# The second half of an output projection, computed one token tile at a time ahead of an expert gather

## The chip, the cores and the metric

One core of a Trainium2 chip runs the whole kernel. Its engines are TensorE (PE: matmuls and, as PEld, weight loads), VectorE (DVE), ScalarE (ACT), GpSimd (POOL) and SyncE (SP, which here only issues transfers). Each engine works through its own queue strictly in order, and semaphores tie the queues together. The metric is device time in microseconds (us). Times in the rows are counted from the start of the profiled span.

## The reference

Two transformer-like blocks follow each other on 256 tokens of 1024 features. The end of the first block is what matters here:

```python
x = x + mixed @ w_out[l]                                  # output projection, 1024 x 1024
x = x + peer_ffn(rmsnorm(x, norm2_gain[l]), peer_w_query[l], ...)
# peer_ffn, for blocks of 128 tokens:
q = (xb @ w_query).reshape(t, 8, 2, 64)                   # 8 heads, two half queries each
s = einsum('thpd,hpkd->thpk', q, sub_keys)                # scores against 128 keys per half
top_s, top_i = top_k(s, 16)                               # 16 best of each half,
best_s, best_pos = top_k(sums of all pairs, 16)           # then the 16 best pairs
u, vv = expert_down[idx], expert_up[idx]                  # 16 rows of 1024 each, per token and head
out = (softmax(best_s) * gelu(xb . u)) @ vv
```

For every token and head, 16 rows of `expert_down` and `expert_up` are fetched from memory, at places known only once the token's scores are sorted. So the fetch of the first head's experts needs the whole row of x for its 128 tokens: the output projection, the norm, the first queries, the scores and the sort.

## The kernel before, in words

The 256 tokens are two tiles of 128 tokens (tile 0 and tile 1 below). Activations are kept transposed (features on partitions) as pairs of rounded halves, `hi` and `lo`. A float32 product is three matmuls (`mm3`, L122: `lh x rl`, `ll x rh`, `lh x rh`). Weights come from memory in chunks of 512 KB, two slices of 128 features by 512 columns. A chunk lands in a buffer `raw` (pool `st`, three buffers), ACT rounds it into `hi` (L106) and DVE writes the difference into `lo` (L110). When DVE has done so, the `raw` buffer is free for SP's next transfer. `stream` (L112) puts `hi` and `lo` into small rings (four and three buffers), which matmuls have to release. These transfers and splits carry a high priority in the scheduler that orders each engine's queue at compile time; equal priorities keep the order of the program.

The stretch around the change runs in this order. `mix_b` ends the first stage (context c1) and writes `mTh`, `mTl`, the input of the output projection. Context c2 then opens its pools `gp`, `wp` and `rt` in the memory that c1's pool gives back. In `gp` lies a ring of ten buffers of 8 KB a partition (`ring`, L697, tag "ga"). Two of them hold the transposed x (`rTh`, `rTl`), four hold the split first half of the query weights (`wh`, `wl`), and the expert rows are gathered into the same ten buffers as they come free.

The output projection (L703 to L707) goes by halves of 512 columns, n = 0 and n = 1. For each half, four chunks of `w_out` are streamed, each used for both token tiles: 48 matmuls of 128x512 a half. VectorE adds the sums to x, and `n2.half(n)` (L224) transposes the four new feature slices of both tiles (L215), writes `rTh` on ACT (L220) and `rTl` on DVE (L221), and has ACT square x for the norm (L247). After n = 1, `n2.factor` (L250) makes the norm factor of both tiles, a chain of small DVE instructions. The split of the query weights' first half (L711 to L717, four chunks of `peer_wq`) keeps its parts in the ring.

Then `lower(0)` (L849) computes tile 0's first queries with 24 matmuls, and `queries` copies them (L732), transposes them (L735) and copies them again (L736). `scores(0, 0)` (L745, L747) and `route(0, 0)` (L752 to L789, on DVE) follow, up to the first list of indices, `idx`. From then on POOL issues indirect gathers of 1 MB (L824), 256 in all, sixteen for each of eight heads and two tiles. `lower(1)`, the second half of the query weights (L866 to L877) and the other scores run beside the first gathers. Each gathered row block is used by a dot product on DVE (L831) and by two matmuls (L840), and then its buffer is free. `after(a, b)` is an edge for the scheduler alone: `a` is queued behind `b` on the same engine.

`tile_part` (L230), which the kernel uses later for the second block's norm, does the transposing and splitting for one token tile and four feature slices, through one PSUM bank.

Of the kernel before, what the change touches and what calls it, by code (L numbers as in the profile page):

```python
# [10 lines left out]
F32 = mybir.dt.float32  # L11
# [6 lines left out]
ALU = mybir.AluOpType  # L18
# [3 lines left out]
P = 128  # L22
D = 1024
KD = D // P
EPS = 1e-6
NEG = -1.0e30
PRIO = 100000
# [4 lines left out]
RAWB, HIB, LOB = 3, 4, 3  # L32
# [15 lines left out]
def peer_hybrid_kernel(ctx: ExitStack, tc: tile.TileContext, A: dict, out: bass.AP, dbg=None, stop=None):  # L48
    nc = tc.nc
    V, S, G, T = nc.vector, nc.scalar, nc.gpsimd, nc.tensor  # L50
    dbg = dbg or {}

    def dump(name, ap):
        if name in dbg:
            nc.gpsimd.dma_start(dbg[name], ap)

    kp = ctx.enter_context(tc.tile_pool(name="kp", bufs=1))
    st = ctx.enter_context(tc.tile_pool(name="st", bufs=1))
    ps = ctx.enter_context(tc.tile_pool(name="ps", bufs=4, space=PSUM))

    def bank(tag="sm"):
        return ps.tile([P, 512], F32, tag=tag, name=tag, bufs=4 if tag == "acc" else 2)
# [8 lines left out]
    x = kp.tile([P, 2, D], F32, name="x", tag="xs")  # L71
# [7 lines left out]
    ident, iota = cst[:, 0], cst[:, 1]  # L79
# [16 lines left out]
    def after(later, earlier):  # L96

        tc.add_manual_dep(later.ins, earlier.ins.name, mybir.DependencyInfo(
            mybir.DependencyClass.NoSync, mybir.DependencyReason.DATA))
# [5 lines left out]
    def split(dst_h, dst_l, src, eng=None):  # L105
        S.activation(dst_h, src, AF.Copy)  # L106
        if eng is None:
            eng = lo_pat[0][cnt[0] % len(lo_pat[0])]
            cnt[0] += 1
        return (V if eng == "v" else G).tensor_tensor(dst_l, src, dst_h.bitcast(F32), op=ALU.subtract)  # L110
# [11 lines left out]
    def mm3(o, lh, ll, rh, rl, start, stop, behind=None):  # L122
        m = T.matmul(o, lh, rl, start=start, stop=False)  # L123
        if behind is not None:
            after(m, behind)
        T.matmul(o, ll, rh, start=False, stop=False)  # L126
        return T.matmul(o, lh, rh, start=False, stop=stop)  # L127
# [38 lines left out]
    def proj_tok(*a, **kw):  # L166
        for _ in proj_tok_steps(*a, **kw):
            pass
# [17 lines left out]
    def rsqrt(dst, ss, inv_n, pool, tag):  # L186
        n = ss.shape[-1]
        shp = list(ss.shape)
        v = pool.tile(shp, F32, tag=tag + "v", name="rsv", bufs=2)
        a = pool.tile(shp, F32, tag=tag + "a", name="rsa", bufs=2)  # L190
        V.tensor_scalar(v, ss, inv_n, EPS, op0=ALU.mult, op1=ALU.add)
        V.tensor_scalar(dst.bitcast(I32), v.bitcast(I32), 1, None, op0=ALU.logical_shift_right)
        V.tensor_scalar(dst.bitcast(I32), dst.bitcast(I32), -1.0, float(0x5F3759DF), op0=ALU.mult, op1=ALU.add)
        for _ in range(3):
            V.tensor_tensor(a, v, dst, op=ALU.mult)
            V.scalar_tensor_tensor(a, a, -0.5, dst, op0=ALU.mult, op1=ALU.mult)
            V.scalar_tensor_tensor(dst, a, 1.5, dst, op0=ALU.add, op1=ALU.mult)

    class Norm:
# [44 lines left out]
        def square(self, tt, halves=(0, 1)):  # L244
            for hf in halves:
                junk = self.pool.tile([P, 512], BF, tag=self.jt[0], name="junk", bufs=self.jt[1])
                after(S.activation(junk, self.x[:, tt, hf * 512:hf * 512 + 512], AF.Square,  # L247
                                   accum_out=self.ss[:, tt, hf:hf + 1]), self.h)

        def factor(self, squares=(), row=True):  # L250

# [76 lines left out]
    with ExitStack() as c1:  # L328
# [22 lines left out]
        acc = [bank("acc") for _ in range(2)]  # L351
        for kc in range(4):
# [4 lines left out]
            for tt in range(2):  # L357
                s = slice(tt * P, tt * P + P)
                for k2 in range(2):
                    k = kc * 2 + k2  # L360
# [96 lines left out]
        b = bank()  # L457
# [5 lines left out]
        for tt in range(2):  # L463
            head_norm(q[:, tt], 16, 64, qg8, b1, "hq")
            rope(q[:, tt], 16, tt, "q")
            for k4 in range(2):
                b = bank()
# [217 lines left out]
    with ExitStack() as c2:  # L685
# [11 lines left out]
        def ring(name, dt=F32R):  # L697
            return gp.tile([P, 2048], dt, tag="ga", name=name, bufs=GB)


        rTh, rTl = (ring(nm).rearrange("p (k t) -> p k t", k=KD) for nm in ("rTh", "rTl"))
        n2 = Norm(x, par("g2"), rt, rTh, rTl)
        for n in range(2):  # L703
            cs_ = slice(n * 512, (n + 1) * 512)
            proj_tok(A["w_out"], n, mTh, mTl, KD,
                     lambda tt, a: V.tensor_tensor(x[:, tt, cs_], x[:, tt, cs_], a, op=ALU.add))
            n2.half(n)  # L707
        n2.factor(row=False)
        dump("x2", x)

        wh, wl = ([ring(f"{nm}{i}") for i in range(2)] for nm in ("wh", "wl"))  # L711
        for kc in range(4):
            raw = st.tile([P, 1024], F32, tag="raw", name="raw", bufs=RAWB)
            o = slice(kc % 2 * 1024, kc % 2 * 1024 + 1024)
            with tc.high_priority(offset=PRIO):
                nc.sync.dma_start(raw, A["peer_wq"][0, kc])
                split(wh[kc // 2][:, o], wl[kc // 2][:, o], raw, "v")  # L717


        idx = [[wp.tile([P, 16], I32, name=f"idx{tt}{h}") for h in range(8)] for tt in range(2)]  # L720
        gate = [[wp.tile([P, 16], F32, name=f"gate{tt}{h}") for h in range(8)] for tt in range(2)]
# [7 lines left out]
        def queries(tt, n, acc):  # L729

            q_ = rt.tile([P, 512], F32, name="q_", bufs=1)
            S.activation(q_, acc, AF.Copy)  # L732
            b = bank()
            for u in range(4):
                T.transpose(b[:, u * P:(u + 1) * P], q_[:, u * P:(u + 1) * P], ident)  # L735
            S.activation(qqT[:, n * 4:n * 4 + 4, tt * P:(tt + 1) * P], b.rearrange("p (h t) -> p h t", h=4), AF.Copy)  # L736

        def scores(tt, n):

            for p_ in range(2):  # L740
                b = bank()
                pr = slice(p_ * 64, p_ * 64 + 64)
                for u in range(4):
                    h = n * 4 + u
                    m = T.matmul(b[:, u * P:(u + 1) * P], qqT[pr, h, tt * P:(tt + 1) * P], keys[pr, h], start=u == 0,  # L745
                                 stop=u == 3)
                c = S.activation(sc[tt][:, n * 4:n * 4 + 4, p_], b.rearrange("p (h k) -> p h k", h=4), AF.Copy,  # L747
                                 scale=n2.r[:, tt:tt + 1])
            return m, c
# [94 lines left out]
        def normalised(tt):  # L844
            xa = S.activation(xn[:, tt], x[:, tt], AF.Copy, scale=n2.r[:, tt:tt + 1])
            after(V.tensor_tensor(xn[:, tt], xn[:, tt], g2r, op=ALU.mult), first)
            return xa

        def lower(tt, behind=None):  # L849
            a = bank("acc")  # L850
            s_ = slice(tt * P, tt * P + P)
            for k in range(KD):
                o = slice(k % 4 * 512, k % 4 * 512 + 512)
                mm3(a, rTh[:, k, s_], rTl[:, k, s_], wh[k // 4][:, o], wl[k // 4][:, o], k == 0, k == KD - 1, behind)
            queries(tt, 0, a)


        lower(0)
        with tc.high_priority(offset=PRIO):
            s0, known = scores(0, 0)  # L860
        with tc.high_priority(offset=PRIO):
            first = route(0, 0, sc[0])
        after(normalised(0), known)
        lower(1, s0)
        acc = [bank("acc") for _ in range(2)]
        for kc in range(4):  # L866
# [449 lines left out]
```

## Time and profile before

| what | value |
|---|---|
| time before, median of 3 runs | 1348.73 us (1348.51 to 1352.42) |
| the profiled execution | 1345.1 us, with a span of 1343.3 us |
| PE, DVE busy over the span | 88%, 67% |
| ACT, POOL busy over the span | 38%, 38% |
| HBM traffic | 285 GB/s over the span |
| expert gathers (queue q0) | 268.45 MB of 383.56 MB moved |

The profiled execution is one run of the program on the chip. In a timeline row the columns are the start, the duration, the engine, the line of the kernel, the operation, its output and inputs by the program's names, and in brackets how long the engine sat idle before it and what ended that wait. In a row of a stretch the columns are the stretch and its length, each engine's busy time with the count of its instructions, the granted clock of TensorE as a share of full speed, the busy share of the transfer engines, and GB/s. SPq and ACTq are the transfers that SP and ACT issue.

### The profile page before, as it was taken

To read this page: it belongs to the slowest core of one execution; us is meant where nothing else is said; L and a number is where in the kernel's file an instruction comes from. 1 tells how busy PE (TensorE), PEld (TensorE's weight loads), DVE (VectorE), ACT (ScalarE), POOL (GpSimd) and SP (SyncE) were. 2 spreads that over 40 slices of the span, in tenths; PEclk is the share of its full clock that TensorE was granted. 3 is DMA by queue.
4 is the path that set the end of the run, shared out by engine and by line. 5 is a ranking of instruction groups with operands and counts; after the bars stand their busy time and mean duration, and the time that the engine had idled before them with its cause. 6 is when DMAs were issued, how large, how long until landed. Compare 5 with 4: busy or idle time off the path is not lost.

```text
span 1343.3 us, 16519 instructions
## 1 busy us (share of the span) xinstructions
PE 1180.3 (88%) x5707; PEld 816.2 (61%) x5707; DVE 894.0 (67%) x1980; ACT 515.4 (38%) x933; POOL 516.8 (38%) x374
## 2 busy tenths in 40 slices
PE   8999999988787778678778777887999999899998
PEld 6977789965333333233333333333888999899987
DVE  6955848677766677776767776665799786635431
ACT  6565535453222122222222222211674564544442
POOL 3322313014454444444445445452100012287964
PEclk9999999989899999999898889889999999999999
DMA  6544425639999999999999999999645346465664
GB/s 217 179 160 128 137 83 163 226 128 427 427 426 427 427 427 427 427 425 427 394 426 427 418 416 426 421 422 385 193 155 172 110 125 192 139 188 179 200 207 136
DMA packets 69779, 383.56 MB, mean 286 GB/s; under 512 B 8000, under 2 KB 8512, under 8 KB 36928
## 3 DMA queue, kind: packets, MB, share of 16 engines
q0 software_dynamic: 36864, 268.45, 47.7%
q1 hardware_dynamic: 31968, 112.15, 27.0%
q10 hardware_dynamic: 864, 1.90, 0.4%
q8 instruction: 46, 0.75, 0.2%
q14 instruction: 37, 0.30, 0.1%
HBM read 381.42 MB, written 1.05 MB: 285 GB/s over the span
## 4 chain that ended last, share of the span: by engine, by line
PE 44%; DMA 26%; DVE 16%; POOL 6%; issue 6%; ACT 2%; POOLq 0%; SPq 0%; DVEq 0%; ACTq 0%
DMA ga<-in_peer_du_dram,idx 23%; PE acc L123 11%; PE acc L126 11%; PE acc L127 11%; DVE jk L831 6%; POOL ga L824 4%; PE acc L840 2%; POOL lo L110 2%; PE sm L1133 1%; PE sm L126 1%; DMA raw<-in_w_fu_dram 1%; PE sm L123 1%; PE sm L127 1%; ACT hi L106 1%; DVE lo L110 1%
## 5 line engine op out<-in xcount | busy, mean ns | idle before, releaser
L840 PE MATMUL acc<-ga,dg 128*128 128x512 f32 x1024 | 489.8, 636 | 132.5 <-ACT dg L837 132.4
L840 PEld LDWEIGHTS acc<-ga,dg 128*128 128x128 f32 x1024 | 203.6, 203 | 416.8 <-issue 236.8
L824 POOL DMA_INDIRECT ga<-in_peer_du_dram,idx x256 | 297.3, 1161 | 386.9 <-PE acc L840 213.9
L831 DVE SCALAR_TENSOR_TENSOR jk<-ga,xn 128x1024 bf16<-128x1024 f32 x253 | 309.4, 1223 | 179.0 <-DMA ga<-in_peer_du_dram,idx 178.6
L106 ACT ACTIVATE hi<-raw 128x1024 fp32r<-128x1024 f32 (+1 forms) x202 | 212.2, 1053 | 235.3 <-PE acc L127 62.7
L110 POOL TENSOR_TENSOR lo<-raw,hi 128x1024 fp32r<-128x1024 f32 (+1 forms) x68 | 166.2, 2449 | 353.3 <-PE acc L127 208.8
L110 DVE TENSOR_TENSOR lo<-raw,hi 128x1024 fp32r<-128x1024 f32 (+1 forms) x134 | 176.7, 1320 | 122.1 <-ACT hi L106 44.0
L123 PE MATMUL acc<-T1l,hi 128*128 128x256 f32 x384 | 107.6, 281 | 2.1 <-DVE T1l L241 2.1
L126 PE MATMUL acc<-T1h,lo 128*128 128x256 f32 x384 | 107.8, 281 | 0.0
L127 PE MATMUL acc<-T1h,hi 128*128 128x256 f32 x384 | 106.9, 279 | 0.0
L123 PE MATMUL acc<-lo,T1h 128*128 128x512 f32 (+1 forms) x256 | 99.2, 395 | 3.1 <-DVE lo L110 1.7
L126 PE MATMUL acc<-hi,T1l 128*128 128x512 f32 (+1 forms) x256 | 99.8, 390 | 0.8 <-DVE T1l L221 0.8
L127 PE MATMUL acc<-hi,T1h 128*128 128x512 f32 (+1 forms) x256 | 99.2, 388 | 0.0
L123 PEld LDWEIGHTS acc<-T1l,hi 128*128 128x128 f32 x384 | 72.2, 188 | 3.0 <-DVE T1l L241 2.4
L126 PEld LDWEIGHTS acc<-T1h,lo 128*128 128x128 f32 x384 | 72.3, 188 | 1.1 <-issue 1.0
L127 PEld LDWEIGHTS acc<-T1h,hi 128*128 128x128 f32 x384 | 72.1, 188 | 0.4 <-issue 0.2
L123 PEld LDWEIGHTS acc<-lo,T1h 128*128 128x128 f32 x256 | 48.1, 189 | 14.0 <-DVE lo L110 2.4
L126 PEld LDWEIGHTS acc<-hi,T1l 128*128 128x128 f32 x256 | 48.5, 190 | 11.0 <-issue 1.1
L127 PEld LDWEIGHTS acc<-hi,T1h 128*128 128x128 f32 x256 | 48.5, 190 | 9.9 <-issue 0.3
L126 PE MATMUL sm<-fhTh,lo 128*128 128x256 f32 x176 | 49.3, 281 | 0.1
L123 PE MATMUL acc<-fhTl,hi 128*128 128x256 f32 x176 | 48.4, 279 | 1.0 <-DVE fhTl L221 1.0
L127 PE MATMUL sm<-fhTh,hi 128*128 128x256 f32 x176 | 49.2, 280 | 0.0
(870 smaller groups left out, 1935.1 us busy)
## 6 DMA issues: line engine op xcount, KB each, us to landing
raw<-in_w_in_dram SPq DMA_DIRECT2D x92, 512.0 KB, 3.6
raw<-in_w_fg_dram SPq DMA_DIRECT2D x22, 512.0 KB, 3.7
raw<-in_w_fu_dram SPq DMA_DIRECT2D x22, 512.0 KB, 3.6
raw<-in_w_fd_dram SPq DMA_DIRECT2D x22, 512.0 KB, 3.7
raw<-in_w_out_dram SPq DMA_DIRECT2D x16, 512.0 KB, 4.4
raw<-in_w_ba_dram SPq DMA_DIRECT2D x8, 512.0 KB, 3.5
raw<-in_w_bm_dram SPq DMA_DIRECT2D x8, 512.0 KB, 3.7
raw<-in_peer_wq_dram SPq DMA_DIRECT2D x8, 512.0 KB, 4.4
```

The source lines that it names most:

```text
L106: S.activation(dst_h, src, AF.Copy)
L110: return (V if eng == "v" else G).tensor_tensor(dst_l, src, dst_h.bitcast(F32), op=ALU.subtract)
L123: m = T.matmul(o, lh, rl, start=start, stop=False)
L126: T.matmul(o, ll, rh, start=False, stop=False)
L127: return T.matmul(o, lh, rh, start=False, stop=stop)
L824: G.indirect_dma_start(ga, None, A["peer_du"], bass.IndirectOffsetOnAxis(idx[tt][h][:, r0 + j:r0 + j + 1], 0))
L831: dot = V.scalar_tensor_tensor(jk, ga[:, 0:D], 1.0, xn[:, tt], op0=ALU.mult, op1=ALU.mult, accum_out=s_[:, j:j + 1])
L840: T.matmul(uacc[tt][dh], dg[:, j], rows[j][:, D + dh * 512:D + dh * 512 + 512], start=h + r0 + j == 0, stop=h == 7 and r0 + j == 15)
L1133: T.matmul(b[:, tt * 4 + m], xl_[:, m, tt], xr_[:, m, tt, :, 1], start=tt + m == 0, stop=tt + m == 4)
```

## The change

The first half of the output projection, n = 0, stays as it is. After it:

- the four chunks of the query weights come first on SP's queue, and `n2.half(0)` stands behind them;
- the second half of `w_out` is no longer streamed through the small rings. Its four chunks are split into four more buffers of the ring of ten (`oh`, `ol`) and stay there;
- `outs(0)` multiplies tile 0 alone (24 matmuls), and `summed(0)` adds it to x, transposes and splits tile 0's four slices by `tile_part`, and squares them. `factor_of(0)` makes tile 0's norm factor;
- `lower(0)`, now at high priority, gives tile 0's first queries. Tile 1's 24 matmuls (`outs(1)`) are queued in three parts: slice 0 behind the last matmul of `lower(0)`, slice 1 behind the transposes of the queries, slices 2 to 7 behind the last matmul of the scores;
- `summed(1)` follows, without an edge (its argument `behind` is not used in it); `factor_of(1)` is queued behind `first`, the cast that writes the first index list; then `lower(1)` as before.

```diff
+        def factor_of(self, tt, behind=None):
+            s = self.pool.tile([P, 2], F32, tag="nst", name="nst", bufs=1)[:, 0:1]
+            a = V.tensor_tensor(s, self.ss[:, tt, 0:1], self.ss[:, tt, 1:2], op=ALU.add)
+            if behind is not None:
+                after(a, behind)
+            rsqrt(self.r[:, tt:tt + 1], s, 1.0 / D, self.pool, "n")
...
+        oh, ol = ([ring(f"{nm}{i}") for i in range(2)] for nm in ("oh", "ol"))
         rTh, rTl = (ring(nm).rearrange("p (k t) -> p k t", k=KD) for nm in ("rTh", "rTl"))
         n2 = Norm(x, par("g2"), rt, rTh, rTl)
-        for n in range(2):
-            cs_ = slice(n * 512, (n + 1) * 512)
-            proj_tok(A["w_out"], n, mTh, mTl, KD,
-                     lambda tt, a: V.tensor_tensor(x[:, tt, cs_], x[:, tt, cs_], a, op=ALU.add))
-            n2.half(n)
-        n2.factor(row=False)
+        proj_tok(A["w_out"], 0, mTh, mTl, KD,
+                 lambda tt, a: V.tensor_tensor(x[:, tt, 0:512], x[:, tt, 0:512], a, op=ALU.add))
...
+        n2.half(0)
+        for kc in range(4):
+            raw = st.tile([P, 1024], F32, tag="raw", name="raw", bufs=RAWB)
+            o = slice(kc % 2 * 1024, kc % 2 * 1024 + 1024)
+            with tc.high_priority(offset=PRIO):
+                nc.sync.dma_start(raw, A["w_out"][1, kc])
+                split(oh[kc // 2][:, o], ol[kc // 2][:, o], raw, "v")
+        oacc = [bank("acc") for _ in range(2)]
+        def outs(tt, ks, behind=None):
+            s_ = slice(tt * P, tt * P + P)
+            for k in ks:
+                o = slice(k % 4 * 512, k % 4 * 512 + 512)
+                m = mm3(oacc[tt], mTh[:, k, s_], mTl[:, k, s_], oh[k // 4][:, o], ol[k // 4][:, o], k == 0, k == KD - 1,
+                        behind)
+            return m
+        def summed(tt, behind=None):
+            V.tensor_tensor(x[:, tt, 512:1024], x[:, tt, 512:1024], oacc[tt], op=ALU.add)
+            n2.tile_part(tt, 1)
+            n2.square(tt, (1,))
+        outs(0, range(KD))
+        with tc.high_priority(offset=PRIO):
+            summed(0)
+            n2.factor_of(0)
...
-        lower(0)
+        with tc.high_priority(offset=PRIO):
+            low, low_t = lower(0)
+        outs(1, (0,), low)
+        outs(1, (1,), low_t)
         with tc.high_priority(offset=PRIO):
             s0, known = scores(0, 0)
+        outs(1, range(2, KD), s0)
+        summed(1, known)
         with tc.high_priority(offset=PRIO):
             first = route(0, 0, sc[0])
         after(normalised(0), known)
+        n2.factor_of(1, first)
         lower(1, s0)
```

`queries` now returns its last transpose and `lower` the last matmul with it, for these edges.

## Rows read from the trace of the kernel before

**Rows 1.** The page: the span, and the transfer engines' busy tenths in 40 slices.
```profile
span 1343.3 us, 16519 instructions
DMA  6544425639999999999999999999645346465664
```
**Rows 2.** Five stretches, all engines.
```profile
251.70:262.70 11.00, 11.00 (x51) 9.10 (x51) 8.28 (x12) 5.35 (x6) 0.00 (x0) 1.00 0.73 240
262.70:274.50 11.80, 11.80 (x58) 9.78 (x57) 7.73 (x11) 6.69 (x12) 0.00 (x0) 1.00 0.61 213
282.20:294.90 12.70, 8.71 (x48) 6.78 (x48) 9.76 (x47) 8.72 (x13) 0.00 (x0) 0.96 0.00 0
297.20:300.70 3.50, 3.50 (x8) 2.81 (x9) 3.50 (x5) 0.00 (x0) 2.75 (x3) 0.50 0.86 290
306.00:936.00 630.00, 494.09 (x1088) 210.01 (x1088) 432.26 (x1142) 146.94 (x399) 288.96 (x250) 0.93 1.01 423
```
**Rows 3.** Timeline of POOL, first and ninth gather.
```profile
295.82 1.21 POOL L824 DMA_INDIRECT ga<-in_peer_du_dram,idx  x1 [55.00 <-DVE idx L789]
...
312.02 0.93 POOL L824 DMA_INDIRECT ga<-in_peer_du_dram,idx  x1 [4.70 <-PE acc L127]
```
**Rows 4.** Timeline of PE: projection, tile 0's queries, transposes, second half of the queries.
```profile
251.74 0.40 PE L123 MATMUL acc<-lo,T1h 128*128 128x512 f32 x1
...
274.46 0.39 PE L123 MATMUL acc<-wl,rTh 128*128 128x512 f32 x1
...
277.19 1.03 PE L215 MATMUL sm<-cst,x 128*128 128x128 f32 x8
...
297.19 0.80 PE L123 MATMUL acc<-lo,rTh 128*128 128x512 f32 x1 [4.16 <-DVE lo L872]
```
**Rows 5.** Timeline of ACT, PE and DVE, from tile 0's queries to the first index list.
```profile
282.18 0.60 ACT L732 ACTIVATE q__3102<-acc 128x512 f32<-128x512 f32 x1 [0.99 <-PE acc L127]
...
282.83 0.66 PE L735 MATMUL sm<-cst,q__3102 128*128 128x128 f32 x4 [0.69 <-ACT q__3102 L732]
...
284.18 1.71 PE L745 MATMUL sm<-keys,qqT 64*128 64x128 f32 x16 [0.69 <-ACT qqT L736]
...
294.70 0.17 DVE L789 CAST idx<-cd__3155 128x16 int32<-128x16 f32 x1
```
**Rows 6.** Timeline of ACT and DVE: weight splits, and where one stage gives way to the next.
```profile
254.93 1.06 ACT L106 ACTIVATE hi<-raw 128x1024 fp32r<-128x1024 f32 x1 [0.35 <-DMA raw<-in_w_out_dram]
...
257.68 0.33 ACTq L690 DMA_DIRECT2D keys<-in_peer_keys_dram  x1
258.12 1.06 ACT L106 ACTIVATE hi<-raw 128x1024 fp32r<-128x1024 f32 x1 [1.54 <-DVE T1l L310]
...
256.96 0.69 DVE L310 SCALAR_TENSOR_TENSOR T1l<-gt,T1h 128x512 fp32r<-128x512 f32 x1
257.56 1.22 DVE L110 TENSOR_TENSOR lo<-raw,hi 128x1024 fp32r<-128x1024 f32 x1
...
276.43 1.22 DVE L110 TENSOR_TENSOR wl<-raw,wh 128x1024 fp32r<-128x1024 f32 x1 [0.27 <-ACT wh L106]
```
**Rows 7.** The buffers `raw` from 235 to 300 us: transfer times.
```profile
DMA to landing us min/median/max: 3.4/4.4/6.8
```
**Rows 8.** Timeline of PE, ACT and DVE: `tile_part` where the kernel uses it later.
```profile
629.26 0.66 PE L235 MATMUL sm<-cst,x 128*128 128x128 f32 x4
...
948.33 0.62 ACT L240 ACTIVATE T1h<-sm 128x128 fp32r<-128x128 f32 x2 [0.17 <-DVE T1l L241]
949.12 0.63 ACT L240 ACTIVATE T1h<-sm 128x128 fp32r<-128x128 f32 x2 [0.16 <-DVE T1l L241]
...
948.73 0.61 DVE L241 SCALAR_TENSOR_TENSOR T1l<-sm,T1h 128x128 fp32r<-128x128 f32 x2 [0.18 <-ACT T1h L240]
```
**Rows 9.** Timeline of DVE: adding the projection, first and last instruction of the norm factor.
```profile
275.48 0.68 DVE L706 TENSOR_TENSOR x<-x,acc 128x512 f32<-128x512 f32 x1
...
281.22 0.16 DVE L255 TENSOR_TENSOR nst<-nss 128x2 f32<-128x2 f32 x1 [0.87 <-ACT junk L247]
...
283.60 0.16 DVE L197 SCALAR_TENSOR_TENSOR nr<-rsa,nr 128x2 f32<-128x2 f32 x1
```

More of the change, by code (lines that the diff above doesn't have):

```diff
@@ L698, in ring @@
             return gp.tile([P, 2048], dt, tag="ga", name=name, bufs=GB)
+        oh, ol = ([ring(f"{nm}{i}") for i in range(2)] for nm in ("oh", "ol"))
         rTh, rTl = (ring(nm).rearrange("p (k t) -> p k t", k=KD) for nm in ("rTh", "rTl"))
         n2 = Norm(x, par("g2"), rt, rTh, rTl)
-        for n in range(2):
-            cs_ = slice(n * 512, (n + 1) * 512)
-            proj_tok(A["w_out"], n, mTh, mTl, KD,
-                     lambda tt, a: V.tensor_tensor(x[:, tt, cs_], x[:, tt, cs_], a, op=ALU.add))
-            n2.half(n)
-        n2.factor(row=False)
-        dump("x2", x)
+        proj_tok(A["w_out"], 0, mTh, mTl, KD,
+                 lambda tt, a: V.tensor_tensor(x[:, tt, 0:512], x[:, tt, 0:512], a, op=ALU.add))
         wh, wl = ([ring(f"{nm}{i}") for i in range(2)] for nm in ("wh", "wl"))
@@ L734, in queries @@
             for u in range(4):
-                T.transpose(b[:, u * P:(u + 1) * P], q_[:, u * P:(u + 1) * P], ident)
+                t = T.transpose(b[:, u * P:(u + 1) * P], q_[:, u * P:(u + 1) * P], ident)
             S.activation(qqT[:, n * 4:n * 4 + 4, tt * P:(tt + 1) * P], b.rearrange("p (h t) -> p h t", h=4), AF.Copy)
+            return t
         def scores(tt, n):
@@ L853, in lower @@
                 o = slice(k % 4 * 512, k % 4 * 512 + 512)
-                mm3(a, rTh[:, k, s_], rTl[:, k, s_], wh[k // 4][:, o], wl[k // 4][:, o], k == 0, k == KD - 1, behind)
-            queries(tt, 0, a)
-        lower(0)
+                m = mm3(a, rTh[:, k, s_], rTl[:, k, s_], wh[k // 4][:, o], wl[k // 4][:, o], k == 0, k == KD - 1, behind)
+            return m, queries(tt, 0, a)
+        with tc.high_priority(offset=PRIO):
+            low, low_t = lower(0)
+        outs(1, (0,), low)
+        outs(1, (1,), low_t)
         with tc.high_priority(offset=PRIO):
             s0, known = scores(0, 0)
+        outs(1, range(2, KD), s0)
+        summed(1, known)
         with tc.high_priority(offset=PRIO):
```

## The prediction

> **What bounds the kernel now.** I read the page first. From about a fifth to seven tenths of the span the transfer engines are full [rows 1]. The stretch table says the same of the expert gathers: from 306 to 936 us the transfer share is 1.01 at 423 GB/s, while TensorE shows a granted clock of 0.93 and idle time [rows 2]. That stage moves a fixed number of bytes at a full rate. So it ends as much earlier or later as it starts, and the question is when it starts. POOL's timeline answers: the first gather is issued at 295.82, after 55 us in which POOL waited for the first index list [rows 3]. The list is written at 294.70 [rows 5]. Everything that the change moves lies on the path to that cast or beside it.
>
> Back from there, tile 0's query copy starts at 282.18, and 12.52 us of copies, transposes, scores and sorting follow [rows 5]. Ahead of it TensorE is the limit: in 251.70 to 274.50 it is busy all the time at a clock of 1.00 [rows 2], with 96 projection matmuls from 251.74 until the query matmuls begin at 274.46 [rows 4]. Weights arrive in time; the transfer share in those two stretches is 0.73 and 0.61 [rows 2].
>
> One matmul of 128x512 costs 0.2275 us in a stream: twelve query matmuls go from 274.46 to the transposes at 277.19 [rows 4]. The 0.39 in their rows is mostly overlap.
>
> **The change, part by part.** Removed from the path are tile 1's 24 matmuls of the second half, 24 x 0.2275 = 5.5 us, tile 1's four slices and its squares. If TensorE stayed the limit, that would be the gain. I think it does not, because the weights become late.
>
> *The weights.* Before the query copy, the path still needs eight chunks after the first half's four: four of the query weights, and now last, four of `w_out`. Their parts no longer wait for matmuls to free a small ring, but they still pass through three `raw` buffers: a transfer, ACT's rounding, DVE's difference, then the next transfer. One such turn is 4.4 us of transfer (median) [rows 7] + 1.06 + 1.22 [rows 6] = 6.7 us for three chunks, 2.2 us a chunk. With the shortest transfer, 3.4 us [rows 7], it is 1.9. What the kernel before achieved for its last eight chunks, with ring waits and queue order in it, is from 257.56 to 276.43 in seven steps [rows 6], 2.7 us a chunk. I take 2.2, and 1.9 and 2.7 as ends.
>
> [...]
>
> *Where the eight begin.* In the kernel before, the first of the eight goes into the small ring and is rounded at 254.93 [rows 6]. Now it goes into a buffer of context c2. The first instruction that touches that context's pools, the transfer of the keys, is issued at 257.68, right after the last instruction of the stage before ends (256.96 + 0.69), and ACT's rounding behind it, at 258.12, is shown waiting for that same instruction [rows 6]. So I let the first rounding start at 258.12: +1.06 + 1.22 = 260.4 for the first chunk, and the eighth is ready at 260.4 + 7 x 2.2 = 275.8 (ends: 273.7 and 279.3).
>
> *From the last chunk to the query copy.* Six matmuls with the overlap of the last one: 1.5. The addition to x: 0.68 [rows 9]. Four transposes: 0.66 [rows 8]. Then four slices: where the kernel uses `tile_part` today, ACT and DVE take turns on the bank, one turn each 0.79 us (948.33 to 949.12, each behind the other) [rows 8]; 4 x 0.79 = 3.2. The last two query matmuls: 0.6. Hand-overs, five at 0.05: 0.25. Together 6.9 us, and the query copy starts at 282.7 instead of 282.18: +0.5 (ends: -1.6 and +4.0). The other twelve query matmuls, and the eighteen of `outs(0)` before the last chunk, fit into TensorE's waits.
>
> [...]
>
> *Queries and sort.* Tile 1's first two slices, three matmuls (0.68 us) each, are queued ahead of the query transposes and of the scores. TensorE idles 0.69 us at both places [rows 5], so they cost nothing; each would cost up to 0.3 us if they start late. The other eighteen run beside the sort, 4.1 us from 285.9. Then the addition for tile 1 (0.68) and its four DVE slices (about 0.31 each) become ready while DVE, in order, works on the sort. Nothing holds them behind it. All five inside would delay the index list by 1.9 us, none by 0. The rows do not tell how many the scheduler lets in; I take 1.0.
>
> *What is hidden.* `factor_of(1)` is a new chain on DVE behind the index cast, 2.5 us long like the one for both tiles today (281.22 to 283.76) [rows 9]. Behind it wait the normalised rows, the query splits and the first dot products. Its cover is the gathers in flight: the first eight need only free buffers. If the cover is too thin it costs up to 2.5; I take 0. All ten ring buffers are now taken when the gathers start, not six. The four of `oh` and `ol` are free once `outs(1)` ends, about 290, before the first gather, and `wh` and `wl` serve the next four as now; the ninth waits for the queries' second half today too (312.02) [rows 3]. On SP only the order of eight transfers changes. POOL has nothing ahead of its first gather.
>
> *The sum.* +0.5 + 1.0 = +1.5 us at the first gather and, since the gathers run at a full rate, at the end. Ends: -1.6 and +4.0 + 1.9 = +5.9, and +8.4 with the late factor chain. The profiled execution took 1345.1 us, of which the span is 1343.3 [rows 1], so it would be 1346.6. The median of the runs shown is 3.6 us above that execution: 1350.2 us, +0.1%. From no change a measurement of this kernel tells 0.3%, 4.0 us, so this is "no change".
>
> **The rivals.** *The weights keep up.* Then TensorE stays the limit: after 262.7 come 36 matmuls (8.2), eight transposes (1.03) [rows 4] and the 5.4 us from the addition on, and the query copy starts at 277.3, 4.9 us earlier; with nothing let into the sort the time is 1343.8. For it: transfers use only 0.61 to 0.73 of their rate now, and the splits no longer wait for matmuls. Against it: it needs some 1.4 us a chunk, and a turn through three buffers has never been under 5.7.
>
> *The weights stay as slow as before.* At 2.7 us a chunk the eighth is ready at 279.3; +4.0 + 1.0 gives 1353.7, slower. It decides from 2.6 us a chunk on. For it: this is what the eight chunks took before, and the splits now share ACT and DVE with the first half's slices. Against it: part of the 2.7 was waiting for matmuls and for TensorE's order, which goes.
>
> [...]
>
> **How the numbers follow.** My forecast has a chance of 0.66, weights that keep up 0.14, weights as slow as before 0.13, the clock 0.07. So faster by over 0.3%: 0.14; within: 0.66; slower: 0.20. The forecast's own range is 1347.1 to 1354.6. To hold 8 in 10 it reaches down into the first rival, and up past the two slower ones: 1344.3 to 1355.5.
>
> **What would show it.** In the changed kernel's timeline, the first `wh` rounding stands at or behind 257.7, and the last `ol` split ends near 276, about 2.2 us a chunk. TensorE then shows waits between 262.7 and 276 that it does not have now. The query copy starts near 282.7, DVE instructions of tile 1 stand between those of the first sort, and the first gather is issued near 297.3. The gather stage is as long as before. I am wrong if the last split ends before 273 or after 278, if the clock in 262 to 283 is not 1.00, or if the gathers run dry after their start.

## The result and the profile after

The changed kernel takes 1357.45 us (median of 7 runs, 1354.25 to 1361.96), the kernel before 1348.73 (7 runs): a ratio of 1.0058, 95% interval 1.0038 to 1.0078. It is slower by 8.7 us, where +1.5 was forecast, and lies above the stated range (1344.3 to 1355.5). The profiled execution took 1356.56.

Two rows of its page, span and transfers, against [rows 1]: the first slices of the gathers are no longer full.

```profile
span 1354.7 us, 16540 instructions
...
DMA  7554425727999999999999999999655336556564
```

Stretches of the changed kernel, columns as in [rows 2]:

```profile
269.80:275.10 5.30, 5.29 (x13) 4.14 (x14) 3.52 (x5) 3.55 (x7) 0.00 (x0) 0.50 0.87 268
310.00:320.00 10.00, 4.45 (x17) 3.25 (x16) 9.62 (x42) 1.20 (x2) 4.62 (x4) 0.81 1.00 409
320.00:330.00 10.00, 7.53 (x37) 6.25 (x36) 7.58 (x21) 5.90 (x11) 2.33 (x2) 0.67 1.01 422
330.00:340.00 10.00, 10.00 (x25) 5.50 (x24) 5.22 (x11) 2.88 (x8) 1.88 (x2) 0.67 0.40 144
350.00:936.00 586.00, 453.51 (x957) 188.22 (x956) 403.28 (x1073) 133.33 (x363) 271.95 (x238) 0.94 1.01 425
```

The clock is 0.50 ahead of the first queries, the transfers run at 144 GB/s in 330 to 340, and from 350 on the stage is as before. So the loss lies between 264 and 340. POOL's gathers 1, 2, 8, 9 and 11:

```profile
300.89 4.61 POOL L855 DMA_INDIRECT ga<-in_peer_du_dram,idx  x1 [59.41 <-PE acc L123]
305.81 0.94 POOL L855 DMA_INDIRECT ga<-in_peer_du_dram,idx  x1 [0.30 <-issue]
...
313.60 1.94 POOL L855 DMA_INDIRECT ga<-in_peer_du_dram,idx  x1 [0.30 <-issue]
322.55 1.23 POOL L855 DMA_INDIRECT ga<-in_peer_du_dram,idx  x1 [7.01 <-PE acc L126]
...
336.46 0.94 POOL L855 DMA_INDIRECT ga<-in_peer_du_dram,idx  x1 [11.28 <-PE acc L871]
```

The first gather starts 5.07 us later than in [rows 3] and takes 4.61 us to issue instead of 1.21. The ninth comes 10.5 us later, and the eleventh waits 11.28 us for the first expert matmuls. TensorE (transposes, first matmul of the second half, its end, fourth part of the second query weights, first experts):

```profile
264.78 0.87 PE L215 MATMUL sm<-cst,x 128*128 128x128 f32 x6 [0.49 <-DVE x L714]
269.81 0.76 PE L123 MATMUL acc<-ol,T1h 128*128 128x512 f32 x1 [4.16 <-issue]
...
280.37 0.39 PE L127 MATMUL acc<-oh,T1h 128*128 128x512 f32 x1
...
317.21 0.80 PE L123 MATMUL acc<-lo,rTh 128*128 128x512 f32 x1 [5.55 <-DVE lo L909]
...
332.41 9.21 PE L871 MATMUL acc<-ga,dg 128*128 128x512 f32 x16
```

VectorE (last split of the weights, tile 1's addition, index list, normalised rows, three differences, first dot, fourth difference):

```profile
274.64 1.23 DVE L110 TENSOR_TENSOR ol<-raw,oh 128x1024 fp32r<-128x1024 f32 x1 [1.14 <-ACT oh L106]
...
294.35 0.68 DVE L741 TENSOR_TENSOR x<-x,acc 128x512 f32<-128x512 f32 x1
...
299.77 0.16 DVE L820 CAST idx<-cd__3159 128x16 int32<-128x16 f32 x1
299.85 1.22 DVE L877 TENSOR_TENSOR xn<-xn,g2r 128x1024 f32<-128x1024 f32 x1
300.98 3.49 DVE L909 TENSOR_TENSOR lo<-raw,hi 128x1024 fp32r<-128x1024 f32 x3
...
310.01 1.23 DVE L862 SCALAR_TENSOR_TENSOR jk<-ga,xn 128x1024 bf16<-128x1024 f32 x1 [4.82 <-DMA ga<-in_peer_du_dram,idx]
...
315.94 1.22 DVE L909 TENSOR_TENSOR lo<-raw,hi 128x1024 fp32r<-128x1024 f32 x1
```

ScalarE (first rounding, tile 0's query copy, tile 1's normalised rows, and the first diagonals, which are the identity scaled by a token's expert weights and go into the expert matmuls):

```profile
257.87 1.06 ACT L106 ACTIVATE wh<-raw 128x1024 fp32r<-128x1024 f32 x1 [1.10 <-DVE T1l L318]
...
286.18 0.60 ACT L762 ACTIVATE q__3066<-acc 128x512 f32<-128x512 f32 x1 [0.60 <-PE acc L127]
...
324.35 1.15 ACT L876 ACTIVATE xn<-x,nr 128x1024 f32<-128x1024 f32 x1
...
330.25 1.27 ACT L868 ACTIVATE dg<-cst,s__3346 128x128 f32<-128x128 f32 x4
```

The loss has three parts. (1) The query copy is 4.0 us later than in [rows 5], and the sort another 1.07. (2) The first gather's issue takes 3.4 us more. (3) VectorE, in order, waits for that gather's rows (4.82 us); the fourth difference, which does not need them and whose rounding on ScalarE ends at 306.81, stands behind the first dots and starts at 315.94, so TensorE waits 5.55 us and goes on at the half clock (0.50 in 317.20 to 322.50). The first expert matmul, which frees the ring, follows the first gather by 31.5 us (before: 19.9), and the transfers run dry.

### The profile page after: what moved, and what is told of

It is laid out like the page before. It is cut to its first block, busy times and chain, and to the rows that moved or that the text cites. A ratio compares the mean times of both kernels' runs of the same rounds, so it can differ in the third digit from the quotient of the medians.

```text
span 1354.7 us, 16540 instructions
## 1 busy us (share of the span) xinstructions
PE 1186.8 (88%) x5707; PEld 821.1 (61%) x5707; DVE 889.2 (66%) x1997; ACT 518.1 (38%) x937; POOL 512.6 (38%) x374
## 3 DMA queue, kind: packets, MB, share of 16 engines
q1 hardware_dynamic: 31968, 112.15, 26.7%
## 4 chain that ended last, share of the span: by engine, by line
PE 46%; DMA 29%; DVE 15%; issue 5%; POOL 3%; ACT 1%; SPq 0%; POOLq 0%; ACTq 0%; DVEq 0%
DMA ga<-in_peer_du_dram,idx 28%; PE acc L123 11%; PE acc L126 11%; PE acc L127 11%; DVE jk L862 5%; POOL ga L855 3%; PE acc L871 2%; PE sm L123 2%; PE sm L126 2%; PE sm L127 1%; DVE lo L110 1%; PE sm L1170 1%; DMA raw<-in_w_in_dram 1%; DVE ti L789 1%; DVE ti L786 1%
## 5 line engine op out<-in xcount | busy, mean ns | idle before, releaser
L106 ACT ACTIVATE hi<-raw 128x1024 fp32r<-128x1024 f32 (+1 forms) x198 | 208.6, 1055 | 226.2 <-PE acc L127 63.0
L126 PE MATMUL acc<-hi,T1l 128*128 128x512 f32 (+1 forms) x240 | 92.8, 387 | 1.1 <-DVE T1l L221 1.1
L123 PE MATMUL acc<-lo,T1h 128*128 128x512 f32 (+1 forms) x240 | 92.1, 391 | 1.6 <-DVE lo L110 1.0
L127 PE MATMUL acc<-hi,T1h 128*128 128x512 f32 (+1 forms) x240 | 92.4, 386 | 0.0
L123 PEld LDWEIGHTS acc<-lo,T1h 128*128 128x128 f32 x240 | 44.8, 188 | 11.7 <-DVE lo L110 1.8
L126 PEld LDWEIGHTS acc<-hi,T1l 128*128 128x128 f32 x240 | 45.1, 188 | 10.6 <-DVE T1l L221 1.3
L127 PEld LDWEIGHTS acc<-hi,T1h 128*128 128x128 f32 x240 | 45.1, 188 | 9.1 <-issue 0.3
L123 PE MATMUL sm<-fhTl,hi 128*128 128x256 f32 x176 | 48.8, 281 | 0.0
```

## The experiments

All edits are to the changed kernel. Executions drift by some us before the stretch (from 255.43 to 259.99 us in these profiles), so the table counts from the end of the last instruction of the stage before (VectorE's `T1l`, L318; L310 in the kernel before). "Held" is the issue of the first gather, "experts" the time from its start to the first expert matmul, GB/s the transfers in the 50 us from its start. Ratios are against the kernel before in the same group of runs (its medians were 1348.73, 1346.66, 1349.04 and 1346.81), with 95% intervals; so versions are compared by ratios, not by times. Apart from the kernel before itself, a row without a ratio is one execution. last_part_first to sort_alone in the table ran on another chip than the other experiments.

| kernel | time, us | ratio | query copy | first gather | held | experts | GB/s |
|---|---|---|---|---|---|---|---|
| before | 1348.73 | | 24.5 | 38.2 | 1.21 | 19.9 | 405 |
| before_again | 1345.2 | | 24.8 | 38.5 | 1.21 | 20.0 | 394 |
| after | 1357.45 | 1.0058 (1.0038 to 1.0078) | 28.3 | 43.1 | 4.61 | 31.5 | 314 |
| after_again | 1354.41 | | 27.5 | 42.2 | 4.61 | 30.6 | 320 |
| queries_first | 1355.51 | 1.0078 (1.0053 to 1.0103) | 27.6 | 42.3 | 4.61 | 29.5 | 331 |
| kept_warm | 1357.89 | 1.0085 (1.0068 to 1.0101) | 27.1 | 41.8 | 4.61 | 30.2 | 319 |
| quiet_first_gather | 1352.86 | | 27.5 | 42.3 | 1.22 | 18.3 | 372 |
| last_part_first | 1351.25 | 1.0013 (0.9992 to 1.0034) | 28.7 | 43.4 | 4.61 | 23.0 | 379 |
| projection_weights_first | 1356.30 | 1.0051 (1.0034 to 1.0069) | 22.3 | 37.0 | 4.61 | 30.4 | 319 |
| both_tiles | 1355.34 | 1.0053 (1.0031 to 1.0074) | 34.3 | 47.9 | 1.20 | 21.0 | 384 |
| sort_alone | 1348.69 | 0.9987 (0.9968 to 1.0007) | 29.4 | 43.0 | 1.80 | 20.3 | 392 |
| sort_alone_again | 1350.00 | 1.0024 (1.0007 to 1.0041) | 27.3 | 40.9 | 1.80 | 20.6 | 398 |
| diagonals_first | 1351.91 | 1.0043 (1.0015 to 1.0072) | 26.7 | 41.4 | 4.61 | 27.7 | 337 |
| both_mended | 1342.74 | 0.9966 (0.9950 to 0.9981) | 23.7 | 37.4 | 1.80 | 22.0 | 381 |

**The two kernels again.** No edit.

> The changed kernel once more, unchanged. It tells whether the two odd sights of its trace belong to the program or to one execution. If they belong to the program: first matmul after the transposes again after about 4.2 us of idle time with the clock at 0.50 behind it, query copy near 286.2, first gather again 4 to 5 us long, transfers dry near 332 to 338. If the long first gather is an accident of one execution: 0.9 to 1.8 us, as the other gathers, and the first dot near 306.6 instead of 310.0.

> The kernel before, profiled once more. Its first profile (1345.1) lies 4 us under the median of its runs. It tells which stage varies: if the start of the gathers and the first matmul of the experts stand where they stood (first gather 38.2 us behind the end of the stage before, first expert matmul 20 us behind the first gather), the spread of some 4 us lies in the long gather stage or behind it, and not in the stretch that the change touches.

Both kernels repeat themselves: 4.61 and 1.21 us to the hundredth, experts at 30.6 and 20.0, and TensorE's wait ahead of the first `w_out` part is 3.65 us instead of 4.16, again with matmuls at the half clock behind it (0.43 us apart). So the three parts belong to the programs. Both profiled executions of the kernel before (1345.1 and 1345.2) lie 1.5 to 4 us under its medians (1346.7 to 1349.0); the profiles of the two kernels differ by 11.4 us, the medians by 8.7.

**The order ahead of the first queries: queries_first.**

```diff
+        half0 = slices(qacc, 0, range(4))
-        outs(0, range(KD))
+        outs(0, range(KD), half0)
```

(`slices` is the loop of `lower`; the other four slices follow where `lower(0)` stood.)

> Four slices of tile 0's queries (12 matmuls) are queued ahead of the 24 of outs(0), nothing else moves. Theory 'order and clock' (TensorE waits for the first w_out part while query work is ready, and then runs at the half clock): the first matmul starts near 268.6 instead of 269.8; if the clock is still 0.50 until about 274, outs(0) ends near 279.3 instead of 280.8 and the query copy starts near 284.8 (-1.4); if the shorter idle keeps the clock at 1.00, outs(0) ends at 277.4 (six matmuls behind the last part, 275.9) and the copy starts near 282.7 (-3.5). The first gather moves by the same amount. Rival 'the weights set it': the last part stays at 275.9 and the copy stays at 286.2, no change in time.

TensorE starts early and idles less at a time, 0.91, 0.80 and 0.92 us, but has only four matmuls between these waits, and the stretch that begins with the third is again at the half clock (TensorE's timeline, then the stretch):

```profile
265.74 0.50 PE L123 MATMUL acc<-wl,rTh 128*128 128x512 f32 x1 [0.91 <-ACT rTh L220]
267.03 0.50 PE L126 MATMUL acc<-wh,rTl 128*128 128x512 f32 x1 [0.80 <-DVE rTl L221]
...
268.95 0.80 PE L126 MATMUL acc<-wh,rTl 128*128 128x512 f32 x1 [0.92 <-DVE rTl L221]
```

```profile
268.50:275.00 6.50, 6.05 (x14) 4.81 (x15) 4.36 (x6) 3.63 (x7) 0.00 (x0) 0.51 0.85 269
```

From the last split's end to the query copy it takes 9.6 us, as in after_again (9.6) and after (10.3). This order alone gains nothing, as the clock is at half with it too (0.51).

**The clock: kept_warm.**

```diff
+        spare = bank("s")
+        for _ in range(20):
+            warm_m = T.matmul(spare, mTh[:, 0, 0:P], mTh[:, 0:2].rearrange("p k t -> p (k t)"), start=True, stop=True)
+            after(warm_m, n2.t)
-        outs(0, range(KD))
+        outs(0, range(KD), warm_m)
```

> Twenty extra 128x512 matmuls on mTh, whose results nothing reads, stand behind n2.half(0)'s transposes; the order behind them is as in the changed kernel. They fill the idle 4.2 us (20 x 0.2275 = 4.6). Theory 'clock': the granted clock stays at 1.00 in 266 to 283, the 36 matmuls behind them take 8.2 us instead of 10.9, outs(0) ends near 278.4 and the query copy starts near 283.8 (-2.4), the first gather with it. Rival 'order alone or the weights': the clock makes no difference, copy at 286.2 or, since the extra matmuls end near 270.3, 0.5 later.

The clock stays at 1.00:

```profile
264.80:283.00 18.20, 15.84 (x72) 12.14 (x71) 9.17 (x13) 8.70 (x16) 0.00 (x0) 1.00 0.65 215
```

```profile
271.40 0.47 PE L123 MATMUL acc<-ol,T1h 128*128 128x512 f32 x1 [0.83 <-issue]
...
279.46 0.39 PE L127 MATMUL acc<-oh,T1h 128*128 128x512 f32 x1
```

The 36 matmuls from the first part of `w_out` to the addition take 8.45 us (271.40 to 279.85) instead of 10.95 (269.81 to 280.76), so the clock was worth 2.5 us. The way from the last split (276.45 + 1.23) to the query copy (285.25) shrinks to 7.6 us; in this execution the last split came 1.5 us later, so the first gather gains only 0.4 to 1.3. The time does not fall: behind the first gather nothing changed (319 GB/s).

**The first gather: quiet_first_gather.**

```diff
+        quiet = l1[:, 0:1]
+        with tc.high_priority(offset=PRIO):
+            pause = V.memset(quiet, 0.0)
+            after(pause, first)
+            for _ in range(3):
+                pause = V.tensor_scalar(quiet, quiet, 1.0, None, op0=ALU.mult)
...
-            after(V.tensor_tensor(lo, raw, hi.bitcast(F32), op=ALU.subtract), first)
+            with tc.high_priority(offset=PRIO if kc < 3 else 0):
+                after(V.tensor_tensor(lo, raw, hi.bitcast(F32), op=ALU.subtract), pause)
```

> Three dummy operations on one column and the first instructions of the next sort stand on VectorE ahead of the three 128x1024 differences of the second query weights, so that the first gather is issued beside small operations. (The fourth rounding moves behind the first gelu with it, so the sum of the time is not read.) Theory 'the wide operations on VectorE hold up the gather': its issue takes 0.9 to 1.3 us instead of 4.61, its rows land 4.5 us later as before, and the first dot starts near 306.6 instead of 310.0; the gathers that fall beside the three differences get longer instead. Rival 'the first gather waits for something else (a buffer, its first descriptors, the transfers of the weights)': still 4 to 5 us, first dot near 310.

POOL's first three gathers, and VectorE's normalised rows and three differences:

```profile
299.86 1.22 POOL L855 DMA_INDIRECT ga<-in_peer_du_dram,idx  x1 [58.72 <-PE acc L123]
301.38 0.94 POOL L855 DMA_INDIRECT ga<-in_peer_du_dram,idx  x1 [0.30 <-issue]
302.63 3.63 POOL L855 DMA_INDIRECT ga<-in_peer_du_dram,idx  x1 [0.30 <-issue]
```

```profile
298.82 1.22 DVE L877 TENSOR_TENSOR xn<-xn,g2r 128x1024 f32<-128x1024 f32 x1
...
301.97 3.48 DVE L916 TENSOR_TENSOR lo<-raw,hi 128x1024 fp32r<-128x1024 f32 x3
```

The long issue went to the gather that meets the differences, and it ends 0.81 us behind them (306.26 against 305.45); in the changed kernel 1.03 behind (305.50 against 304.47). So in both kernels one gather beside the wide differences was held up: 4.61 and 3.63 us of issue, against 1.22 and 0.94 for the two that started ahead of it here. What the hold alone costs in time this run doesn't tell, since the order behind it changed too (experts at 18.3, less than in the kernel before). What the rows do not settle: in the kernel before, the same operations stand beside its first gather, which gets in after the first of them.

```profile
294.11 1.22 DVE L846 TENSOR_TENSOR xn<-xn,g2r 128x1024 f32<-128x1024 f32 x1
295.24 3.49 DVE L872 TENSOR_TENSOR lo<-raw,hi 128x1024 fp32r<-128x1024 f32 x3
```

There (before_again) the gather ends at 296.36, 1.03 behind the end of `xn`. In all seven profiles with tile 1's slices inside the first sort and the differences beside the first gather it was held over all three, in the six profiles of before, both_tiles, sort_alone and both_mended it was not. The gather's start does not tell them apart: it stands 0.09 us ahead of the differences in the changed kernel (300.89 and 300.98) and in before_again (295.15 and 295.24). Why it is let in between two operations in one order and not in the other stays open, and no run shows by what the operations hold it.

**The fourth difference: last_part_first.**

```diff
+            with tc.high_priority(offset=PRIO if kc == 3 else 0):
+                last_lo = after2(V.tensor_tensor(lo, raw, hi.bitcast(F32), op=ALU.subtract), first)
...
+                if behind is not None:
+                    after(dot, behind)
...
+                dot = experts(tt, h, r0, nr, last_lo if n + r0 == 0 else None)
```

(`after2` is `after` and returns its first argument.)

> The fourth difference of the second query weights is queued ahead of the first dot products on VectorE (high priority, and the first expert block's dots behind it); nothing else is changed by hand. Theory 'the gathers run dry because TensorE gets the fourth part 8 us late': the difference starts near 310 instead of 315.9, TensorE does not idle 5.6 us and stays at 1.00, the second halves' query copies start near 313 to 316 instead of 320 and 324, gather 9 near 315 instead of 322.6, the first expert matmul near 323 instead of 332, and the transfers no longer stand still at 332 to 338: 5 us less in all (3 to 8). Rival 'the rows land late and ScalarE's order (tile 1's scores ahead of the diagonals) sets the first expert matmul': it stays at 329 or later, the transfers still stand still, and the time is the same within 1.5 us.

VectorE's fourth difference and the last instruction of tile 1's factor, the first expert matmul, and the stretch that was dry:

```profile
311.50 1.22 DVE L916 TENSOR_TENSOR lo<-raw,hi 128x1024 fp32r<-128x1024 f32 x1
...
313.77 0.15 DVE L201 SCALAR_TENSOR_TENSOR nr<-rsa,nr 128x1 f32<-128x1 f32 x1
```

```profile
324.84 15.38 PE L877 MATMUL acc<-ga,dg 128*128 128x512 f32 x32
```

```profile
330.00:340.00 10.00, 10.00 (x24) 4.18 (x22) 5.10 (x9) 1.48 (x5) 6.65 (x6) 1.00 1.02 429
```

A new order on VectorE takes the standstill away, though the first gather is as late and as long as in the changed kernel. By the ratios it is worth 6 us (1.0013 against 1.0058, intervals apart). What 379 GB/s is short of 405 in 50 us is 3.2 us, about the hold. The rival falls. The theory holds for the queue, but not for the fourth difference alone: with the edit the next sort and most of tile 1's factor also came ahead of the first dot (the factor ends at 313.92 instead of 321.74), and no run parts them.

**ScalarE's order: diagonals_first.** Tile 1's scores, tile 0's second scores and `normalised(1)` get an edge behind the first block's diagonals.

```diff
-        scores(0, 1)
-        for n in range(2):
-            scores(1, n)
...
+                if n + r0 == 0:
+                    for tn in ((0, 1), (1, 0), (1, 1)):
+                        scores(*tn, diag[3])
```

> On ScalarE, tile 1's scores, tile 0's second scores and tile 1's normalised rows are queued behind the first expert block's diagonals; VectorE's order of the fourth difference stays as in the changed kernel (near 316). Theory 'ScalarE's order': with the fourth dot at 321.7 to 323 and a table load behind it, the diagonals start near 325.5 and the first expert matmul near 326 instead of 332.4, the transfers stand still for under 2 us, and the time falls by 4 to 7 us. Rival 'TensorE's late fourth part alone (it was the only thing that last_part_first changed by hand)': the first expert matmul waits for the queries anyway and stays at 330 or later, the time falls by under 2.

It gets halfway: experts at 27.7 instead of 31.5, because the fourth part still reaches TensorE late, and the standstill moves and shrinks (TensorE, then the stretches):

```profile
313.23 0.79 PE L123 MATMUL acc<-lo,rTh 128*128 128x512 f32 x1 [5.58 <-DVE lo L913]
```

```profile
320.00:330.00 10.00, 9.21 (x28) 5.57 (x29) 7.49 (x13) 5.80 (x11) 2.35 (x2) 0.66 0.80 337
330.00:340.00 10.00, 9.29 (x47) 5.52 (x46) 3.43 (x6) 3.79 (x9) 3.23 (x4) 1.00 0.89 342
```

So both queues take part, and the edit on VectorE moves the experts more. In time the 4 to 7 us expected are not shown: 1.0043 against 1.0058, with intervals that overlap.

**The order of the weights: projection_weights_first.** The two loops of transfers and splits change places (w_out's second half ahead of the query weights).

> The two groups of four transfers and splits change places: w_out's second half first, the query weights behind it, all else as in the changed kernel. Theory 'what stands behind the last weights counts, not how many bytes': the eighth part is still ready near 276, but only six query matmuls stand behind it instead of projection, addition, transposes, four slices and queries, so the query copy starts near 277.5 instead of 286.2 (278.5 at the half clock), the first gather near 292, 8.5 us earlier, and the time falls by as much, to that of the kernel before, if the gathers behind run dry as before; the first gather may then be held up or not. Rival 'TensorE's order and the slices set it': copy not before 282, the time at most 4 us less.

```profile
280.19 0.60 ACT L762 ACTIVATE q__3066<-acc 128x512 f32<-128x512 f32 x1 [0.59 <-PE acc L127]
```

```profile
294.90 4.61 POOL L855 DMA_INDIRECT ga<-in_peer_du_dram,idx  x1 [53.84 <-PE acc L123]
```

The query copy comes at 280.19, 22.3 behind the stage before: 6.0 us earlier than in the changed kernel and 2.2 earlier than before, though not the 8.7 expected. The first gather starts earlier than in the kernel before, and yet the time stays at +0.5%: held 4.61, experts 30.4, 319 GB/s. So the start alone did not decide. A start 6.1 us earlier than in the changed kernel is not paid back one to one either: 1.0051 against 1.0058, which the intervals do not tell apart.

**The split by tiles: both_tiles.** Weights kept and in the changed kernel's order, both tiles together again (`n2.half(1)`, `n2.factor`).

> The weights stay in the ring and come in the changed kernel's order, but the second half is computed for both tiles together again, with n2.half(1) and one norm factor as in the kernel before. It parts the two halves of the change. Theory 'the order of the weights costs the start, the tile split costs the gathers': 48 matmuls stand where 24 stood, so the query copy starts near 288 (5.5 us of matmuls more, 1.3 less for slices over two banks, tile 1 nowhere in the way), the sort takes 8.8 us again instead of 9.8, the first gather is issued near 302, and the gathers run dry less, as tile 1's factor is there early; time +9 to +12 over the kernel before. Rival 'the tile split is what costs': copy, first gather and time fall back to those of the kernel before, within 3 us.

As expected in its parts, if not in size: the query copy stands 9.8 us later than before (expected some 6), the sort takes as long as before, and the gathers are fed well (held 1.20, experts 21.0). In time it stays below what was expected, about 7 us over the kernel before instead of 9 to 12. The 1.3 us less for slices over two banks was an estimate of mine, and no run shows it: from ScalarE's first slice to VectorE's last, the eight of both tiles took 2.42 us here (287.23 to 289.65), tile 0's four 3.11 in the changed kernel (282.24 to 285.35). projection_weights_first is its counterpart: an earlier start, and the gathers as dry as in the changed kernel. So the weights' order, with the weights kept in the ring, costs the start, and the split by tiles costs the gathers. POOL's first gather in both_tiles:

```profile
305.06 1.20 POOL L858 DMA_INDIRECT ga<-in_peer_du_dram,idx  x1 [64.33 <-DVE idx L823]
```

**Tile 1 out of the first sort: sort_alone and sort_alone_again.**

```diff
+            add = V.tensor_tensor(x[:, tt, 512:1024], x[:, tt, 512:1024], oacc[tt], op=ALU.add)
+            if behind is not None:
+                after(add, behind)
...
-        summed(1, known)
         with tc.high_priority(offset=PRIO):
             first = route(0, 0, sc[0])
+        summed(1, first)
```

> Tile 1's addition and slices are queued behind the first index list on VectorE. Theory 'sort': the 1.06 us that they took inside the first sort go, the sort takes 8.8 us and the first gather is issued 1.0 earlier; tile 1's queries and factor come some 3 us later, and the gathers run dry for longer, so that the time does not fall, or rises by up to 3 us. Rival 'the first gather alone counts': time -1.

> The kernel of sort_alone again, against the same runs of the kernel before as both_mended, for a narrower interval: -0.4 us was measured (ratio 0.9968 to 1.0007), where its first gather stood 4.8 us later than in the kernel before. If the start counts one to one, the ratio lies near 1.003; if it is the same time again, a later start of the gathers by some 5 us is made good somewhere, and the profile has to show where.

From query copy to first gather it takes 13.6 us, as in the kernel before (changed kernel: 14.7): the 1.07 is gone. But the larger effect was not expected. The first gather is held 1.80 only, and the scheduler now puts the first experts ahead of tile 1's second queries on TensorE, so the ring frees early. POOL's first gather, TensorE's first experts, and the stretch:

```profile
299.95 1.80 POOL L857 DMA_INDIRECT ga<-in_peer_du_dram,idx  x1 [57.24 <-DVE x L741]
```

```profile
320.53 7.13 PE L873 MATMUL acc<-ga,dg 128*128 128x512 f32 x16
```

```profile
330.00:340.00 10.00, 9.98 (x41) 5.56 (x41) 5.01 (x9) 3.66 (x9) 2.99 (x3) 1.00 1.01 426
```

"Dry for longer" was wrong, and with it the time that was expected: it falls, from 1.0058 to 0.9987 and 1.0024. The gain can't be given to the sort alone, since the hold and TensorE's order changed with it. In the second group, start +2.7 and hold +0.6 make +3.3; measured were +3.2. In the first group, -0.4 was measured at a start of +4.8; the two intervals touch only at 1.0007. The rows do not explain the difference, so the fit in the second group proves little; the two groups ran on two chips, and whether that matters is not shown.

**Both edits together: both_mended.**

> projection_weights_first and sort_alone together. If their effects add: the query copy stands 22 us behind the end of the stage before (24.5 in the kernel before), the sort takes 8.8, the first gather is issued 36.0 us behind it instead of 38.2 in the kernel before and is not held up longer than 1.8 us, the first expert matmul follows some 20 us later and the transfers never stand still. Then the time is 1 to 3 us under the kernel before. Rival 'an earlier start is given back, because TensorE gets tile 1's slices, queries and scores all behind the first gather': first expert matmul over 23 us behind the first gather and the same time as sort_alone, within 1.5 us.

The version is faster than the kernel before, and by the ratios faster than the changed one: ratio 0.9966 (0.9950 to 0.9981), -4.1 us in the medians. Copy and first gather stand 0.8 earlier than in the kernel before. Its profiled execution lies 4.5 us above its median (1347.28) and shows 381 GB/s; from its rows alone a gain of 4 us doesn't follow, so where the rest of it lies stays open.

## Why the prediction was wrong

- *Weights as the limit, 2.2 us a chunk, eighth part at 275.8:* right. The first rounding stands at 257.87, the last split ends at 274.64 + 1.23 = 275.87. The steps between were uneven (roundings 0.97 to 4.60 us apart, 2.24 in the mean); only their sum was forecast well. Of the rivals on the weights neither came.
- *From the last chunk to the query copy, 6.9 us:* it took 10.3. All of the 3.4 us stand in its first term: "Six matmuls with the overlap of the last one", put at 1.5 us, took 4.9 (275.87 to 280.76). The step that failed is "The other twelve query matmuls, and the eighteen of `outs(0)` before the last chunk, fit into TensorE's waits." The first of `outs(0)` stood ahead of the ready query work, TensorE idled 4.16 us, and 13 matmuls then ran at 0.50. Of the 36 ahead of the addition six should have been left when the last part was ready, at 275.87; at 275.36 there were 23 left, 5.2 us of work, and the last began at 280.37. The forecast gave the clock a chance of 0.07; the wait that stood ahead of the half clock came from the queue's order. Of the 3.4 us the half clock is 2.5 by kept_warm, which leaves 0.9 for the order.
- *Four slices by turns of 0.79:* right (282.24 to 283.02 to 283.81). *Sort +1.0:* 1.07, but this was a guess between 0 and 1.9 that no row supported (the addition and three of the four slices were let in), so partly luck.
- *What is hidden, 0:* wrong, and the larger error. "Its cover is the gathers in flight: the first eight need only free buffers" is true of the issue, but the eleventh gather needs the first expert matmul, and that stood behind the fourth difference, tile 1's second queries, the late factor (its last instruction at 321.58) and tile 1's scores. last_part_first shows it: 6 us back from VectorE's order alone. 314 instead of 405 GB/s over 50 us from the first gather is 11.2 us; 3.4 of it is the hold, and the 7.8 left I put down to the standstill.
- *"POOL has nothing ahead of its first gather":* true of POOL's queue, but the issue itself was held beside VectorE's differences (4.61 us instead of 1.21), which no term of the sum had.
- *One to one from the first gather to the end:* not in the medians. Start +5.1, hold 3.4 and standstill 7.8 make 16.3; at the end of the gathers (x's addition behind them, kernel before and changed kernel below) 14.4 of it is left, in the spans 11.4, in the medians 8.7. In all ten rows of the table with a ratio, the later start plus what the 50 us are short of 405 GB/s comes to 0.4 to 7.4 us more than the medians differ by. So the rows name the parts and do not price them; where the rest goes is not shown.

```profile
943.10 0.69 DVE L897 TENSOR_TENSOR x<-x,acc 128x512 f32<-128x512 f32 x1
```

```profile
957.53 0.69 DVE L934 TENSOR_TENSOR x<-x,acc 128x512 f32<-128x512 f32 x1
```

I had written that I would be wrong if the clock in 262 to 283 was not 1.00 or the gathers ran dry after their start. Both happened; the only price that I had near the second, 2.5 us for a late factor chain, I took as 0.

## What to carry to other kernels

When a change moves work to just behind the start of a long transfer-bound stage, follow each engine's queue up to the instruction that frees the stage's buffers for the first time: moving a few ready instructions on VectorE ahead of a wait on the first rows gave back some 6 us here, while a first gather 6.1 us earlier gave back no more than the noise. Price a TensorE wait together with what its queue has ready behind the waiting matmul, and with the half clock that followed it here (13 matmuls at 0.50 behind 4.16 us). And check which wide VectorE operations stand beside the first indirect gather: three of them held it for 3.4 us here.

## What the runs showed of the hardware

- Three back-to-back 128x1024 differences on VectorE held an indirect gather for 3.4 us in seven profiles (those with 4.61 in the table): its issue took 4.61 us, and ended 1.03 us behind them in the changed kernel. In six others with the same three beside it (before, before_again, both_tiles, sort_alone, sort_alone_again, both_mended) it took 1.20 to 1.80 us and ended 1.02 or 1.03 us behind the 128x1024 operation ahead of the three. With operations of 128 columns and fewer in their place it took 1.22 (quiet_first_gather).
- In the changed kernel TensorE's granted clock was 0.50 behind idle times of 4.16 and 5.55 us; in queries_first it was 0.51 behind waits of 0.91, 0.80 and 0.92 us with four matmuls between them. With 20 matmuls in the gap (kept_warm) it stayed at 1.00.
